# A two-layer streaming encoder on one core: select scratch and recurrence operands in PSUM, conditioning blocks moved

## Chip, cores and metric

The kernel runs on one core of one Trainium2 chip. The metric is the device time of one execution in microseconds (us), median of the runs; lower is better. The profile comes from one execution, recorded by the hardware profiler.

## What is computed

A prompt of 256 tokens and a sample of 32 tokens go through two layers of width 1024: a gated linear recurrence (layer 0) and a convolution module (layer 1), each followed by a PEER mixer that picks 16 of 16384 experts per head and token. Every part is normalised and modulated by a conditioning vector c. Cut to what matters:

```python
def rglru_block(h, ...):
    gate_branch, rec_branch = jnp.split(h @ w_in + b_in, 2, axis=-1)
    gate = jax.nn.gelu(gate_branch)
    xc = causal_dwconv(...rec_branch...)
    r, i = sigmoid(xh @ ga_w + ga_b), sigmoid(xh @ gx_w + gx_b)   # per head
    a = jnp.exp(-LRU_C * r * softplus(-lam))
    bvals = jnp.sqrt(1 - a * a) * (i * xc)
    hs = associative_scan(a, bvals)              # h[t] = a[t] h[t-1] + bvals[t]
    return (hs * gate) @ w_out + b_out

def peer(h, w_q, k1, k2, u, v):                  # per token, 8 heads
    s1, s2 = q1 @ k1.T, q2 @ k2.T                # 128 keys each
    s1v, s1i = top_k(s1, 16); s2v, s2i = top_k(s2, 16)
    sv, si = top_k(s1v[:, None] + s2v[None, :], 16)
    e = s1i[si // 16] * 128 + s2i[si % 16]
    g = softmax(sv)
    return sum(g * gelu(u[e] . h) * v[e])

for l in range(2):
    sh1, sc1, g1, sh2, sc2, g2 = split(silu(c) @ ada_w[l] + ada_b[l], 6)
    x = x + g1 * block(modulate(rmsnorm(x), sh1, sc1))
    x = x + g2 * peer(modulate(rmsnorm(x), sh2, sc2))
```

## The kernel before

The whole model runs on one core as a stream of items; `run_stream` (line 244) lays out one item per step `n`: a load on the SyncE (SP) queue, a split of the loaded tile into a rounded half `hi` (ScalarE, ACT) and a rest `lo` (VectorE, DVE, or GpSimd, POOL: `split_w`, line 329), and three groups of products on TensorE (PE): hi with both halves of the activations, lo with one (`mm3`, line 336). Splits run one step ahead, transposes of expert tiles two. Everything else (scans, top-16, gates, evictions) is in threads, lists of operations with an engine and a cost. `run_threads` (line 183) lets out as many of them per step as the engine's budget allows; a step's budget is the cost of its items on PE less what the split uses, and a conditioning block adds 0.5. So each engine's queue has a fixed order that the costs settle in advance. `drain_threads` lets out all that is left.

The order of items in layer 0: 16 conditioning blocks; 16 dense items for `w_in` (0 to 7 the recurrent half, 8 to 15 the gate half); 8 for `w_out`; then the PEER mixer: z items 0 to 127 (the product of all experts' `u` with the activations, with 16 query items between z1 and z8) and v items 0 to 127 (`v`). Layer 1 repeats this with its convolution in place of the recurrence. The names used below:

- A conditioning block is 512 KB of `ada_w`, four products with 32 columns of weights and 512 moving columns (`ada_unit`, line 390). Eight blocks make one of the twelve units (layer, part); the last block starts a small thread that transposes the row (ACT, PE) and adds the bias (DVE). `with_ada` hangs blocks behind items (`ride`) or ahead of one (`lead`). Blocks of layer 0's later units use a ring of nine buffers, so a block's load is issued when the block nine before it has been used.
- The recurrence ends in `lru_tail` (line 1368): per channel group c of 128, `ex` and `ex2` (exponential on ACT, square on POOL), `v1` (DVE), `sq` (square root, ACT), `v2` (a product and two scans, DVE), `gelu` (ACT) and `out` (product with the gate, POOL). `pre_wout` drains what is left and makes hi and lo of the result for `w_out`.
- After the query items, `select_ops` (line 738) finds the 16 best of 50 candidate pairs on DVE, turns their positions into two expert indices (`start1`, eight `steps`, `ints`, `start2`, eight `steps`), makes the softmax, and prepares tables for the gates (`tr`, `ev`, `parts`). Its work runs in both halves `hh` of 18 rows of 16. Beside it the z items go on: DVE transposes each tile of `u` (line 955), ACT makes hi, POOL makes lo while gates are open.
- PSUM has two pools of four banks: `bank()` for products, `bank(True)` for accumulators. `scr` and `big` are SBUF.

In `lru_tail` the order among roots and scans stands in these lines:

```python
sops += [("C", 0, lambda c=c: n["v1"] >= min(C, c // 4 * 4 + 4)), ("S", 0.33, lambda c=c: sq(c), 0)]
vops += [("C", 0, lambda c=c: n["sq"] > c), ("V", 0.95, lambda c=c: v2(c), 0)]
```

Of the kernel before, what the change touches and what calls it, by code (L numbers as in the profile page):

```python
# [21 lines left out]
P = 128  # L22
D = 1024
C = 8
# [22 lines left out]
def trunk_kernel(ctx: ExitStack, tc: tile.TileContext, I: dict, O: list):  # L47
# [564 lines left out]
    def peer_items(l, st, x8, sq8, hT8, hp8, rep8, ada_list):  # L612
# [125 lines left out]
        def select_ops():  # L738
            o = 4 * NA
            cand = scr[:, o:o + NH * NCAND].rearrange("p (h k) -> p h k", h=NH)  # L740
            ia, ib = hk(o, NA, I32), hk(o + NA, NA, I32)
            tmp = hk(o + 2 * NA, NA)
# [10 lines left out]
            def in_psum():  # L753
                return bank(True)[:, :NA].rearrange("p (h k) -> p h k", k=TOPK)
            bc = [P, NH // 2, TOPK]
            ops = []

            def add(eng, cost, fn, *hop):
                ops.append((eng, cost, fn) + hop)
# [10 lines left out]
            def conv():  # L770
                far["pos"], far["tmp"] = in_psum(), in_psum()
                for a in hh:
                    V.tensor_copy(far["pos"][:, a], ci[:, a])
                    V.tensor_copy(smx[:, a], sv[:, a, 0])
                for a in hh:
                    V.tensor_tensor(sv[:, a], sv[:, a], smx[:, a].unsqueeze(2).to_broadcast(bc), op=ALU.subtract)
            add("V", 1.1, conv)
            add("S", 0.5, lambda: S.activation(sv, sv, AF.Exp), 1)


            def start1():
                for a in hh:
                    V.tensor_copy(k1[:, a], idxs[0][:, a])
                for a in hh:
                    V.tensor_copy(k2[:, a], idxs[1][:, a])
                for a in hh:
                    V.scalar_tensor_tensor(k1[:, a], k1[:, a], 64.0, offs.unsqueeze(1).to_broadcast(bc),
                                           op0=ALU.mult, op1=ALU.add)
                for a in hh:
                    V.tensor_tensor(dl[:, a, 1:], k1[:, a, 1:], k1[:, a, :15], op=ALU.subtract)  # L790
                for a in hh:
                    V.tensor_copy(i1[:, a], k1[:, a, 0:1].to_broadcast(bc))
# [10 lines left out]
            add("V", 2.1, start1, 0)  # L803
# [3 lines left out]
            def soft():  # L807
                V.tensor_reduce(smx, sv, axis=AX.X, op=ALU.add)
                V.reciprocal(smx, smx)
                for a in hh:  # L810
                    V.tensor_tensor(sv[:, a], sv[:, a], smx[:, a].unsqueeze(2).to_broadcast(bc), op=ALU.mult)
            add("V", 1.2, soft, 0)

            def ints():
                for a in hh:
                    V.tensor_copy(ia[:, a], i1[:, a])
                for a in hh:
                    V.tensor_scalar(ib[:, a], ia[:, a], 63, None, op0=ALU.bitwise_and)
                for a in hh:
                    V.tensor_scalar(ia[:, a], ia[:, a], 6, None, op0=ALU.arith_shift_right)  # L820
                for a in hh:
                    V.tensor_copy(tmp[:, a], ib[:, a])

            def start2():
                for a in hh:
                    V.tensor_copy(i1[:, a], ia[:, a])
                for a in hh:
                    V.tensor_tensor(far["pos"][:, a], far["pos"][:, a], tmp[:, a], op=ALU.subtract)
                for a in hh:
                    V.tensor_tensor(dl[:, a, 1:], k2[:, a, 1:], k2[:, a, :15], op=ALU.subtract)  # L830
                for a in hh:
                    V.tensor_copy(i2[:, a], k2[:, a, 0:1].to_broadcast(bc))
# [5 lines left out]
            gate, man = scr[:, 4 * NP:5 * NP], scr[:, 5 * NP:6 * NP]  # L838
# [9 lines left out]
            def ev(tt):  # L848
                def f():
                    pt = st.pop(("slot", tt))  # L850
                    S.copy(sidx[:, :, tt * P:(tt + 1) * P], pt[:, :2 * P].rearrange("p (n t) -> p n t", n=2))
                    S.copy(gate[:, tt * P:(tt + 1) * P], pt[:, 2 * P:3 * P])
                return f

            def parts():
                V.tensor_copy(iota4, iota.unsqueeze(2).to_broadcast([P, P, 4]))
                V.tensor_scalar(man.bitcast(I32), gate.bitcast(I32), 0x007FFFFF, 0x44800000,
                                op0=ALU.bitwise_and, op1=ALU.bitwise_or)
                V.tensor_scalar(gate.bitcast(I32), gate.bitcast(I32), 0x7F800000, None, op0=ALU.bitwise_and)
                V.tensor_copy(smant[:, 0], man)  # L860
                V.tensor_scalar(sexp, gate, 1.0 / 1024, None, op0=ALU.mult)
# [506 lines left out]
    def lru_tail():  # L1368
# [12 lines left out]

        def sq(c):
            S.activation(ML[:, c, :], ML[:, c, :], AF.Sqrt)
            n["sq"] += 1

        def v2(c):
            V.tensor_tensor(IB[:, c, :], IB[:, c, :], ML[:, c, :], op=ALU.mult)
            V.tensor_tensor_scan(ML[:, c, :NP], RA[:, c, :NP], IB[:, c, :NP], 0.0, ALU.mult, ALU.add)
            V.tensor_tensor_scan(ML[:, c, NP:T], RA[:, c, NP:T], IB[:, c, NP:T], vc("state_lru_h", c),
                                 ALU.mult, ALU.add)  # L1390
            n["v2"] += 1
# [9 lines left out]
        for c in range(C):  # L1401
            sops += [("C", 0, lambda c=c: n["v1"] >= min(C, c // 4 * 4 + 4)), ("S", 0.33, lambda c=c: sq(c), 0)]
# [68 lines left out]
    with_ada(d, a01, {k: 2 for k in range(2, 10)}, {16: (8, 0)})  # L1471
    items += d
    a1 = ada_unit(0, 5, rc) + [it for u in range(2) for it in ada_unit(1, u, rc)]
# [441 lines left out]
```

## Time and profile before

| | us |
|---|---|
| Median of 3 runs | 2060.77 (2055.79 to 2065.05) |
| The profiled execution | 2065.36 |
| its span, first to last instruction | 2063.6 |
| PE busy | 1989.8 (96%) |
| DVE busy | 1534.8 (74%) |
| ACT busy | 1113.3 (54%) |
| POOL busy | 993.7 (48%) |

PE is the fullest engine over the whole span, but the shares are means over stages with different limits. What a change in one stage is worth is read from the windows and timelines of that stage: how much PE works in it, and for whom it waits. A timeline's bracket gives the idle time ahead of an instruction and who ended it; its durations are those of one instruction, or of a run of `x` equal ones. A long instruction can hide a wait of its own. The granted clock (PEclk) is a share of 2.4 GHz.

### The profile page before, as it was taken

Reading aid. Unit: us, or ns where it says so; the run is one execution under the profiler, and the core shown is the slowest. Engines: PE = TensorE matmul, PEld = TensorE weight load, DVE = VectorE, ACT = ScalarE, POOL = GpSimd, SP = SyncE. Lnnn points to the kernel's source line nnn. Section 1 sums busy time; section 2 is a strip of 40 time slices with the busy share of each in tenths; the row PEclk is TensorE's granted clock in tenths of the full one; section 3 lists DMA queues with packets and bytes.
Section 4 is the critical chain, followed back from the end, with each engine's and each line's share of the span. In section 5 each row is a group of like instructions: output and inputs, shape, how many; then the busy total and the mean of one; then the engine's idle time right before and its main releaser. Section 6 shows DMA issues by size and latency. Waiting matters only on the chain.

```text
span 2063.6 us, 38013 instructions
## 1 busy us (share of the span) xinstructions
PE 1989.8 (96%) x13603; PEld 1718.6 (83%) x13603; DVE 1534.8 (74%) x3324; ACT 1113.3 (54%) x1973; POOL 993.7 (48%) x644
## 2 busy tenths in 40 slices
PE   6989999999999999999999899999999999999998
PEld 4777978999999887777877679999999988777776
DVE  5785559999998876455658855799999978754455
ACT  3655434478886444344554544444888854444444
POOL 4346667777775232121245266877777743312100
PEclk9999999999999999999999999999999999999999
DMA  9856595555556988887686455665555578878863
GB/s 341 274 180 217 142 247 163 168 171 158 156 155 220 314 297 284 291 278 235 236 271 163 148 161 147 179 174 164 169 158 155 157 259 315 296 276 293 277 202 124
DMA packets 311483, 444.44 MB, mean 215 GB/s; under 512 B 29326, under 2 KB 248126, under 8 KB 310782
## 3 DMA queue, kind: packets, MB, share of 16 engines
q1 hardware_dynamic: 292142, 374.73, 57.6%
q0 software_dynamic: 18976, 67.22, 9.4%
q8 instruction: 107, 1.75, 0.4%
q14 instruction: 82, 0.67, 0.1%
q10 hardware_dynamic: 176, 0.07, 0.0%
HBM read 434.19 MB, written 4.87 MB: 213 GB/s over the span
## 4 chain that ended last, share of the span: by engine, by line
PE 65%; DVE 11%; issue 9%; DMA 8%; POOL 5%; ACT 2%; SPq 1%; DVEq 0%; ACTq 0%; POOLq 0%
PE b L342 34%; PE acc L1089 21%; DVE ut L955 3%; PE acc L913 3%; POOL scr L996 3%; POOL lo L333 2%; DMA raw<-in_peer_u_dram 2%; DMA raw<-in_peer_v_dram 2%; PE b L1033 1%; DMA big<-in_ada_w_dram 1%; DVE lo L333 1%; ACT hi L332 1%; PE acc L406 1%; DMA scr<-in_peer_u_dram,eidx 1%; DVE acc L798 1%
## 5 line engine op out<-in xcount | busy, mean ns | idle before, releaser
L342 PE MATMUL b<-rnd,hi 128*128 128x256 f32 (+1 forms) x5376 | 737.9, 290 | 19.7 <-ACT hi L332 10.8
L333 POOL TENSOR_TENSOR lo<-ut,hi 128x1024 fp32r<-128x1024 f32 x253 | 608.1, 2406 | 231.7 <-PE b L342 122.2
L342 PEld LDWEIGHTS b<-rnd,hi 128*128 128x128 f32 x5376 | 681.1, 190 | 42.2 <-ACT hi L332 15.8
L332 ACT CAST hi<-raw 128x1024 fp32r<-128x1024 f32 x336 | 353.1, 1052 | 396.7 <-DMA raw<-in_peer_v_dram 234.0
L1089 PE MATMUL acc<-hi,rnd 128*128 128x512 f32 x2048 | 557.6, 393 | 2.9 <-ACT hi L332 2.7
L333 DVE TENSOR_TENSOR lo<-raw,hi 128x1024 fp32r<-128x1024 f32 x282 | 348.1, 1236 | 265.0 <-PE acc L1089 124.7
L1089 PEld LDWEIGHTS acc<-hi,rnd 128*128 128x128 f32 x2048 | 380.2, 188 | 111.9 <-issue 23.4
L955 DVE STREAM_TRANSPOSE ut<-raw 128x1024 f32<-128x1024 f32 x256 | 317.0, 1239 | 129.4 <-DMA raw<-in_peer_u_dram 97.2
L342 PE MATMUL b<-rnd,lo 128*128 128x256 f32 (+1 forms) x2688 | 386.4, 285 | 9.6 <-POOL lo L333 5.2
L342 PEld LDWEIGHTS b<-rnd,lo 128*128 128x128 f32 x2688 | 351.2, 189 | 14.3 <-POOL lo L333 8.8
L332 ACT CAST hi<-ut 128x1024 fp32r<-128x1024 f32 x256 | 269.5, 1053 | 172.2 <-DVE ut L955 148.8
L1089 PE MATMUL acc<-lo,rnd 128*128 128x512 f32 x1024 | 317.7, 391 | 1.7 <-DVE lo L333 1.3
L1089 PEld LDWEIGHTS acc<-lo,rnd 128*128 128x128 f32 x1024 | 191.2, 188 | 46.6 <-DVE lo L333 6.8
L1023 POOL DMA_INDIRECT big<-in_peer_v_dram,eidx x64 | 65.6, 1025 | 266.0 <-PE b L1033 252.8
L333 POOL TENSOR_TENSOR lo<-raw,hi 128x1024 fp32r<-128x1024 f32 x54 | 129.9, 2407 | 113.0 <-PE b L342 60.1
L996 POOL DMA_INDIRECT scr<-in_peer_u_dram,eidx x64 | 84.2, 1316 | 187.3 <-DVE scr L1000 186.6
L907 ACT ACTIVATE scr<-scr 128x128 bf16<-128x128 bf16 x512 | 169.3, 407 | 0.0
L976 ACT ACTIVATE big<-b 128x512 f32<-128x512 f32 (+32 forms) x123 | 59.8, 486 | 73.4 <-PE b L342 73.2
L1000 DVE SCALAR_TENSOR_TENSOR scr<-scr 128x1024 f32<-128x1024 f32 x64 | 78.1, 1221 | 25.9 <-DMA scr<-in_peer_u_dram,eidx 25.7
L1064 DVE TENSOR_TENSOR rnd<-big,rnd 128x512 fp32r<-128x512 f32 x128 | 89.9, 702 | 4.1 <-ACT rnd L1063 4.1
L913 PE MATMUL acc<-scr 128*128 128x128 bf16 x1024 | 81.9, 223 | 0.0
L1063 ACT CAST rnd<-big 128x512 fp32r<-128x512 f32 x128 | 78.8, 615 | 4.0 <-PE b L342 4.0
(316 smaller groups left out, 1593.6 us busy)
## 6 DMA issues: line engine op xcount, KB each, us to landing
raw<-in_peer_u_dram SPq DMA_DIRECT2D x1024, 128.0 KB
raw<-in_peer_v_dram SPq DMA_DIRECT2D x256, 512.0 KB
big<-in_ada_w_dram SPq DMA_DIRECT2D x96, 512.0 KB
raw<-in_peer_w_q_dram SPq DMA_DIRECT2D x128, 128.0 KB
raw<-in_cf_w_pw_dram SPq DMA_DIRECT2D x24, 512.0 KB
raw<-in_lru_w_in_dram SPq DMA_DIRECT2D x16, 512.0 KB
raw<-in_lru_w_out_dram SPq DMA_DIRECT2D x8, 512.0 KB
xsave<-big SPq DMA_DIRECT2D x2, 1152.0 KB
```

Of the source, the lines that this page charges most:

```text
L332: S.copy(hi, src)
L333: (G if pool_lo else V).tensor_tensor(lo, src, hi.bitcast(F32), op=ALU.subtract)
L342: TE.matmul(ps, w[wi][:, c * P:(c + 1) * P], a[ai][:, c, :n], start=(start and wi == c == ai == 0), stop=(stop and wi == 1 and c == C - 1))
L907: S.activation(bt[:, j], b4[:, :, j], AF.Copy, scale=sexp[:, t0 + j:t0 + j + 1])
L913: TE.matmul(s["ps"][:, j * P:(j + 1) * P], a[:, :, j], bt[:, j], start=a is hi, stop=a is lo)
L955: V.transpose(s["ut"].rearrange("p (b e n) -> p e b n", b=8, e=4), s["raw"].rearrange("p (e b n) -> p e b n", e=4, b=8))
L996: G.indirect_dma_start(out=gt, out_offset=None, in_=Uf, in_offset=bass.IndirectOffsetOnAxis(ap=eidx[:, s:s + 1], axis=0))
L1000: V.scalar_tensor_tensor(gt, gt, 1.0, hs_v, op0=ALU.mult, op1=ALU.mult, accum_out=zs[:, s:s + 1])
L1023: G.indirect_dma_start(out=gt[j], out_offset=None, in_=Vf, in_offset=bass.IndirectOffsetOnAxis(ap=eidx[:, s + j:s + j + 1], axis=0))
L1063: S.copy(w[0], src)
L1064: V.tensor_tensor(w[1], src, w[0].bitcast(F32), op=ALU.subtract)
L1089: TE.matmul(acc[tt][half], w[a][:, c0:c0 + P], s["w"][b][:, half * 512:(half + 1) * 512], start=(i == 0 and a == 0 and b == 0), stop=(i == ...
```

## The change

It has three parts.

1. `select_ops`: scratch operands move into the two accumulator banks that the stage already holds (`pos` and `tmp`): the row maxima and the reciprocal sums (`red`), the scaled first index, the integer index (`int`), and later mantissa and exponent (`bits`). The casts of the indices to float go from DVE to ACT, behind the exponential; so does the iota copy of `parts`. The copy of the low index bits to float is dropped. `start1` is let out one step behind `exp` (hop 1).
2. `lru_tail`: `sq` writes its root into a bank of the product pool; `v2` multiplies in place there, and both scans read their second input from it. A root is let out only when the scan two channels before it has been.
3. Two more conditioning units (layer 0 part 5, layer 1 part 0) join the three that ride on the dense items of layer 0: two blocks behind items 2 to 9, 11, 13 and 15, four behind 10, 12 and 14, six instead of eight ahead of `w_out`. Eight blocks instead of 24 are left for the mixer of layer 0.

```diff
 def select_ops():
-            ia, ib = hk(o, NA, I32), hk(o + NA, NA, I32)
-            tmp = hk(o + 2 * NA, NA)
+            ib = hk(o + NA, NA, I32)
...
             def conv():
-                far["pos"], far["tmp"] = in_psum(), in_psum()
+                b0, b1 = bank(True), bank(True)
+                far["pos"], far["tmp"], far["int"] = in_psum(b0), in_psum(b1), in_psum(b1.bitcast(I32))
+                far["red"] = b0[:, NA:NA + NH]
+                far["bits"] = b0[:, :NP], b1[:, :NP]
                 for a in hh:
                     V.tensor_copy(far["pos"][:, a], ci[:, a])
-                    V.tensor_copy(smx[:, a], sv[:, a, 0])
+                    V.tensor_copy(far["red"][:, a], sv[:, a, 0])
                 for a in hh:
-                    V.tensor_tensor(sv[:, a], sv[:, a], smx[:, a].unsqueeze(2).to_broadcast(bc), op=ALU.subtract)
+                    V.tensor_tensor(sv[:, a], sv[:, a], red(a), op=ALU.subtract)
+
+            def exp():
+                S.activation(sv, sv, AF.Exp)
+                for n in range(2):
+                    S.copy(idxf[n], idxs[n])
             add("V", 1.1, conv)
-            add("S", 0.5, lambda: S.activation(sv, sv, AF.Exp), 1)
+            add("S", 1.3, exp, 1)
 
             def start1():
+                t = far["tmp"]
                 for a in hh:
-                    V.tensor_copy(k1[:, a], idxs[0][:, a])
-                for a in hh:
-                    V.tensor_copy(k2[:, a], idxs[1][:, a])
-                for a in hh:
-                    V.scalar_tensor_tensor(k1[:, a], k1[:, a], 64.0, offs.unsqueeze(1).to_broadcast(bc),
+                    V.scalar_tensor_tensor(t[:, a], k1[:, a], 64.0, offs.unsqueeze(1).to_broadcast(bc),
                                            op0=ALU.mult, op1=ALU.add)
                 for a in hh:
-                    V.tensor_tensor(dl[:, a, 1:], k1[:, a, 1:], k1[:, a, :15], op=ALU.subtract)
+                    V.tensor_copy(k1[:, a], t[:, a])
+                for a in hh:
+                    V.tensor_tensor(dl[:, a, 1:], t[:, a, 1:], k1[:, a, :15], op=ALU.subtract)
...
-            add("V", 2.1, start1, 0)
+            add("V", 1.6, start1, 1)
...
             def soft():
                 V.tensor_reduce(smx, sv, axis=AX.X, op=ALU.add)
-                V.reciprocal(smx, smx)
+                V.reciprocal(far["red"], smx)
                 for a in hh:
-                    V.tensor_tensor(sv[:, a], sv[:, a], smx[:, a].unsqueeze(2).to_broadcast(bc), op=ALU.mult)
+                    V.tensor_tensor(sv[:, a], sv[:, a], red(a), op=ALU.mult)
 
             def ints():
+                ia = far["int"]
...
-                for a in hh:
-                    V.tensor_copy(tmp[:, a], ib[:, a])
 
             def start2():
                 for a in hh:
-                    V.tensor_copy(i1[:, a], ia[:, a])
+                    V.tensor_copy(i1[:, a], far["int"][:, a])
                 for a in hh:
-                    V.tensor_tensor(far["pos"][:, a], far["pos"][:, a], tmp[:, a], op=ALU.subtract)
+                    V.tensor_tensor(far["pos"][:, a], far["pos"][:, a], ib[:, a], op=ALU.subtract)
...
             def ev(tt):
...
+                    if tt == 1:
+                        S.copy(iota4, iota.unsqueeze(2).to_broadcast([P, P, 4]))
 
             def parts():
-                V.tensor_copy(iota4, iota.unsqueeze(2).to_broadcast([P, P, 4]))
+                man, ex = far["bits"]
                 V.tensor_scalar(man.bitcast(I32), gate.bitcast(I32), 0x007FFFFF, 0x44800000,
                                 op0=ALU.bitwise_and, op1=ALU.bitwise_or)
-                V.tensor_scalar(gate.bitcast(I32), gate.bitcast(I32), 0x7F800000, None, op0=ALU.bitwise_and)
+                V.tensor_scalar(ex.bitcast(I32), gate.bitcast(I32), 0x7F800000, None, op0=ALU.bitwise_and)
                 V.tensor_copy(smant[:, 0], man)
-                V.tensor_scalar(sexp, gate, 1.0 / 1024, None, op0=ALU.mult)
+                V.tensor_scalar(sexp, ex, 1.0 / 1024, None, op0=ALU.mult)
                 V.tensor_tensor(smant[:, 1], man, smant[:, 0], op=ALU.subtract)
...
 def lru_tail():
+        pb = {}
+
         def sq(c):
-            S.activation(ML[:, c, :], ML[:, c, :], AF.Sqrt)
+            pb[c] = bank()[:, :T]
+            S.activation(pb[c], ML[:, c, :], AF.Sqrt)
             n["sq"] += 1
 
         def v2(c):
-            V.tensor_tensor(IB[:, c, :], IB[:, c, :], ML[:, c, :], op=ALU.mult)
-            V.tensor_tensor_scan(ML[:, c, :NP], RA[:, c, :NP], IB[:, c, :NP], 0.0, ALU.mult, ALU.add)
-            V.tensor_tensor_scan(ML[:, c, NP:T], RA[:, c, NP:T], IB[:, c, NP:T], vc("state_lru_h", c),
+            V.tensor_tensor(pb[c], IB[:, c, :], pb[c], op=ALU.mult)
+            V.tensor_tensor_scan(ML[:, c, :NP], RA[:, c, :NP], pb[c][:, :NP], 0.0, ALU.mult, ALU.add)
+            V.tensor_tensor_scan(ML[:, c, NP:T], RA[:, c, NP:T], pb[c][:, NP:T], vc("state_lru_h", c),
                                  ALU.mult, ALU.add)
...
-            sops += [("C", 0, lambda c=c: n["v1"] >= min(C, c // 4 * 4 + 4)), ("S", 0.33, lambda c=c: sq(c), 0)]
+            sops += [("C", 0, lambda c=c: n["v1"] >= min(C, c // 4 * 4 + 4) and n["v2"] >= c - 1), ("S", 0.33, lambda c=c: sq(c), 0)]
...
-    with_ada(d, a01, {k: 2 for k in range(2, 10)}, {16: (8, 0)})
+
+    a01 += ada_unit(0, 5, rb) + ada_unit(1, 0, rb)
+    with_ada(d, a01, {k: 4 if k in (10, 12, 14) else 2 for k in range(2, 16)}, {16: (6, 0)})
...
-    a1 = ada_unit(0, 5, rc) + [it for u in range(2) for it in ada_unit(1, u, rc)]
+    a1 = ada_unit(1, 1, rc)
```

## Rows read from the trace of the kernel before

**Rows 1.** The page, part 1: busy us, share of span, instructions.

```profile
PE 1989.8 (96%) x13603; PEld 1718.6 (83%) x13603; DVE 1534.8 (74%) x3324; ACT 1113.3 (54%) x1973; POOL 993.7 (48%) x644
```

**Rows 2.** Windows: us, busy by engine (x instructions), clock, DMA share, GB/s.

```profile
260.57:300.22 39.65, 38.97 (x299) 28.92 (x299) 19.77 (x77) 14.61 (x25) 24.89 (x19) 1.00 1.02 261
1290.80:1317.26 26.46, 26.46 (x224) 26.14 (x223) 19.34 (x73) 11.98 (x16) 21.99 (x13) 1.00 0.67 180
```

**Rows 3.** Windows around w_out of layer 0.

```profile
90.00:97.00 7.00, 7.00 (x57) 6.99 (x54) 5.79 (x10) 6.98 (x15) 6.56 (x8) 1.00 0.52 149
97.00:123.20 26.20, 18.23 (x132) 14.16 (x131) 25.85 (x40) 18.05 (x39) 15.62 (x12) 0.99 0.41 121
123.20:130.00 6.80, 6.79 (x41) 6.80 (x42) 4.94 (x15) 2.05 (x5) 0.00 (x0) 0.78 0.30 91
```

**Rows 4.** Timeline of DVE in the recurrence: start, us, line, operation [idle before].

```profile
100.34 0.45 DVE L1387 TENSOR_TENSOR big<-big 128x288 f32<-128x288 f32 x1
100.83 0.69 DVE L1388 TENSOR_TENSOR_SCAN big<-big 128x256 f32<-128x256 f32 x1
101.43 0.26 DVE L1389 TENSOR_TENSOR_SCAN big<-big,vecT 128x32 f32<-128x32 f32 x1
...
102.86 1.20 DVE L333 TENSOR_TENSOR lo<-raw,hi 128x1024 fp32r<-128x1024 f32 x1
...
115.04 2.76 DVE L1388 TENSOR_TENSOR_SCAN big<-big 128x256 f32<-128x256 f32 x1
...
119.45 2.29 DVE L1389 TENSOR_TENSOR_SCAN big<-big,vecT 128x32 f32<-128x32 f32 x1
```

**Rows 5.** Timeline of POOL in the recurrence.

```profile
111.31 0.87 POOL L1398 TENSOR_TENSOR big<-big 128x288 f32<-128x288 f32 x1 [1.36 <-ACT big L1416]
...
118.95 2.72 POOL L333 TENSOR_TENSOR lo<-raw,hi 128x1024 fp32r<-128x1024 f32 x1
```

**Rows 6.** Timeline of PE ahead of w_out.

```profile
115.32 3.64 PE L406 MATMUL acc<-big,scT 128*32 128x512 f32 x32
...
123.20 3.59 PE L342 MATMUL b<-rnd,hi 128*128 128x288 f32 x15 [3.92 <-DVE rnd L496]
```

**Rows 7.** Windows of the select stage: layer 0 in part, whole; layer 1.

```profile
326.00:371.00 45.00, 40.76 (x331) 39.30 (x329) 42.45 (x90) 21.16 (x24) 32.86 (x14) 1.00 0.57 162
326.00:433.00 107.00, 98.78 (x810) 95.86 (x809) 98.90 (x209) 48.96 (x65) 80.05 (x34) 1.00 0.57 164
1345.00:1450.00 105.00, 99.11 (x810) 96.82 (x808) 98.47 (x224) 49.17 (x65) 79.33 (x34) 0.98 0.60 168
```

**Rows 8.** Timeline of PE, select stage: a larger stall, one of ten small.

```profile
341.41 2.15 PE L342 MATMUL b<-rnd,hi 128*128 128x256 f32 x16 [1.86 <-ACT hi L332]
...
347.36 1.20 PE L342 MATMUL b<-rnd,lo 128*128 128x256 f32 x8 [0.32 <-POOL lo L333]
```

**Rows 9.** DVE by line and form, 290 to 450 us: busy us, mean ns.

```profile
L798 DVE SCALAR_TENSOR_TENSOR acc<-acc,scr 128x144 f32<-128x144 f32 x60 | 18.4, 308 | 1.5
...
L776 DVE TENSOR_TENSOR scr<-scr,smx 128x144 f32<-128x144 f32 x2 | 2.7, 1396 | 0.0
...
L818 DVE TENSOR_SCALAR scr<-scr 128x144 int32<-128x144 int32 x2 | 2.6, 1326 | 0.0
...
L859 DVE TENSOR_SCALAR scr<-scr 128x256 int32<-128x256 int32 x1 | 2.4, 2423 | 0.0
L856 DVE CAST scr<-iota 128x512 f16<-128x512 f32 x1 | 1.5, 1548 | 0.0
...
L773 DVE CAST acc<-scr 128x144 f32<-128x144 uint32 x2 | 0.6, 290 | 0.0
...
L783 DVE CAST scr<-scr 128x144 f32<-128x144 uint32 x2 | 0.3, 203 | 0.0
```

**Rows 10.** Windows of the projections ahead of that.

```profile
50.00:75.00 25.00, 25.00 (x170) 19.99 (x169) 22.08 (x47) 16.14 (x34) 10.47 (x21) 1.00 1.06 372
...
70.00:80.00 10.00, 10.00 (x69) 7.68 (x69) 9.47 (x23) 5.38 (x13) 0.95 (x1) 1.00 0.98 318
```

## What the change does to the time, and why

> **What bounds the kernel now.** I read the page's engine shares first: TensorE (PE) is busy 96% of the span [rows 1], so a gain has to come out of the 73.8 us in which PE stands idle, or out of work that PE no longer does. Then the windows, to see where the idle time lies, and for each stretch the timelines of the engines that PE waited for. Three stretches matter. (a) Nine z items behind the query projections of layer 0 carry conditioning blocks; the same nine of layer 1 carry none, and their windows stand side by side: 39.65 against 26.46 us [rows 2]. (b) Between the fifth gate product and w_out of layer 0, PE works 18.23 of 26.20 us, while VectorE (DVE) works 25.85 [rows 3]. The scans are the reason: a clean channel costs 0.45 + 0.69 + 0.26 us, but some scans take 2.76 or 2.29 us, and the last ends just behind a 2.72 us subtraction on GpSimd (POOL) [rows 4, 5]. PE waits 3.92 us for the last lo halves, and behind that wait the granted clock of 6.8 us is 0.78: part of them at the lower of its two levels, 1.2 GHz [rows 3, 6]. (c) In the select stage of both layers DVE is nearly full (42.45 of 45.00 us) and PE loses 8.22 us of 107 in layer 0 and 5.89 of 105 in layer 1, at a clock of 0.98 there [rows 7]. The larger losses stand behind ACT's hi cast, which waits for DVE's transpose; ten smaller ones, 0.3 us each, behind POOL's lo half [rows 8]. Which DVE instructions are long there is seen by line: 144 columns should take about 0.3 us, yet lines 776 and 818 average 1.4 and 1.3 us, and 859 takes 2.42 us for 256 columns [rows 9].
>
> **Part 1, the select stage, twice.** The slow forms are those whose operands all lie in SBUF. Line 798, with its output and first input in PSUM, is issued 60 times between POOL instructions that fill 32.86 of 45.00 us, and averages 308 ns: it never waits [rows 7, 9]. The change puts into PSUM an operand of just the lines that waited: the maxima and reciprocal sums (776, 811), the scaled first index (787, 790), the integers (816, 818, 820, 826), mantissa and exponent (857, 859). It takes the index casts (783, 785) and the copy of line 822 off DVE, and gives ACT those casts and the iota copy (856). In layer 0 that is 2.2 us at 776, 2.2 at 818, 2.1 at 859 and 1.5 at 856: 8 us by these four lines alone [rows 9]. PE can get back no more than it lost: 8.22 + 5.89, and 0.02 x 105 = 2.1 us for the clock, 16.2 us together. The sixteen long steps (lines 798 and 801) stay as they are; the ten small stalls, 3.2 us, are in them, and I let these and a little of the rest stay: **-12 us**. Bounds: -16, and -3 (the waits hop to operations that keep two SBUF operands, lines 830, 832 and 792). What is added: two casts and a copy on ACT, which is busy under half of these windows [rows 7]. Its next hi cast queues behind them, and start1 on DVE waits for them, for which the planner leaves one step (hop 1). I cost that at nothing; were that cover gone, it would be about the 1.5 us a layer that the iota copy took on DVE.
>
> A cast of 144 columns from SBUF to SBUF averages 203 ns, into PSUM 290 ns [rows 9]. The Trainium skill (VectorE: DVE Perf Modes, Why PSUM operands drop a tier) says that fp32 operations of one source lose their doubled rate once an operand is in PSUM; by that rule, with which these rows agree, some fourteen instructions a layer get slower. At 0.09 us each, were all of it on the path, the sum would be 2.4 us worse, but DVE has 8 us to spare by then.
>
> **Part 2, the conditioning blocks.** Sixteen of 24 blocks leave the z items of layer 0; one stays there, behind the seven ahead of the first. The two windows differ by 13.19 us for 17 blocks, with their transposes and two waits for DMA, so 16 blocks are worth 13.19 x 16/17: **-12.4 us** [rows 2]. Bounds -11 and -13.2. Each block takes with it its load on SP, its four products and an eighth of a post thread. The planner grants DVE 0.5 us per block, so without them the select thread runs slower: by the costs written in the code it starts its first top-16 two steps later and ends one step later, as layer 1 does today. The gates then end at z124, still ahead of the first v item, and the sample output one v item later, with room for it.
>
> The blocks go to the gate products: 18 more between items 10 and 15, two fewer ahead of w_out. A block costs PE between 0.45 us (eight in a row take 3.64 us [rows 6]) and 0.78 us (13.19/17, with a change of operand kind and the transposes). Here they come in twos and fours, and I take 0.6: 18 x 0.6 - 2 x 0.45 = 9.9 us. Against that stand 7.97 us of idle PE before w_out and 1.5 us that the clock of 0.78 takes out of the 6.8 us behind it [rows 3]. So PE alone would reach the end of w_out's first item 0.4 us later than today (from -2.3 at 0.45 a block to +3.7 at 0.78).
>
> **Part 3, the recurrence in PSUM.** Product and both scans now read one operand from PSUM, so by the argument of line 798 a channel should cost the clean 1.3 us. From 100.34 to 121.74 us, less three lo halves of 1.2 us, eight channels take 17.8 us today; 8 x 1.3 is 10.4 [rows 4]. DVE gains 7 us, and stops being what w_out waits for. What comes late next is PE with its blocks, then the loads. There is a price in order: root c may be issued only when scan c-2 has been, and ACT takes the gelus after all roots, so by the planner's order six of eight outputs on POOL fall behind the lo half of w_out's first tile and four behind that of its second, which waits for the buffer of the last gate product. After that product come 2.7 us of lo half [rows 5], then four outputs of 0.9 us [rows 5], then cast and lo half, some 7 us in all, and PE has six blocks and six transposes (4 us) to fill it, and its first channels of w_out for 2 us more. It just fits.
>
> **The loads.** In 90 to 123.2 us the DMA moves 149 GB/s x 7 + 121 x 26.2 = 4.2 MB [rows 3]; 16 blocks of 512 KB add 8.4 MB. 12.6 MB take 33.9 us at 372 GB/s, which it held from 50 to 75 us, and 39.6 at the 318 of 70 to 80 us [rows 10], against 33.2: +0.7 to +6.4. The last three blocks can only be asked for when item 14's are used. The Trainium skill (DMA: Bandwidth & Descriptors, Specifications) gives about 358 GB/s of HBM per core; by that figure an estimate is 35.2 us, or +2.0. The rows show more than that, so they decide.
>
> For what happens ahead of w_out together I take **+2 us**, between PE alone (+0.4) and the loads with their late requests; bounds -2.3 and +8.
>
> **The sum.** -12 - 12.4 + 2 = -22.4 us. The profiled execution took 2065.4 us, 4.6 above the median of the runs shown and just over their highest; against itself the sum gives 2043, against the median of 2060.8 it gives 2038.4. I predict **2038 us**.
>
> **The rivals.**
> *The wait moves (chance 0.12).* DVE keeps forms with two SBUF operands, and each can meet a POOL subtraction. For it: of the two instructions of line 776, and of 818, the means of 1.4 and 1.3 us say that only one waited [rows 9], so who waits is a matter of alignment. Against it: few of them are left per layer. Part 1 gives -3: 2047 us.
> *Loads too late (0.10).* If the DMA holds 318 GB/s with column slices and blocks mixed, w_out starts 6.4 us late and its own tiles come late behind it: +10 instead of +2: 2046 us.
> *A PSUM operand frees nothing (0.07).* Then the change doesn't do what it says: part 1 keeps only what leaves DVE (-3), the scans stay long, DVE ends as today at 122 us with two more units to finish, w_out +4: 2049 to 2051 us. Line 798 speaks against it. The Trainium skill (SBUF — State Buffer, Who interferes with whom) has it that a DVE instruction with at most one SBUF input, outside the doubled modes, does not contend with GpSimd; by that rule this rival is dead, and line 798's row agrees.
> *Slower: banks chain the engines (0.05).* Roots and gate products share four PSUM banks. As the steps run, product 13 takes the bank of channel 1, product 14 that of channel 3 and product 15 that of channel 5, each used at least one step before; root 3 waits for scan 0, root 7 for scan 4. If DVE falls more than a step behind, PE waits for scans, these for roots, and these queue on ACT behind evictions that wait for PE. Wholly in series, the stretch would take 25.85 + 18.05 + 18.23 = 62.1 instead of 26.2 us [rows 3], +36, and the sum becomes +11.6: 2072 us. It decides from 24.4 us of loss on. Against it: DVE has 7 us less to do in this stretch and PE 10 us more, so DVE should run ahead.
>
> **How the numbers follow.** My forecast has 0.66. Parts at their good ends give -16 - 13.2 - 2.3 = -31.5 (2029), at bad ends -3 - 11 + 8 = -6 (2055); runs of before spread by 5 us to either side. 2026 to 2052 leaves out the slower case, the worst of the bad ends and little below: two in ten. About 0.5%, or 10.3 us, is what a measurement of this kernel can tell from no change; faster means under 2050.5. Nearly all of the forecast lies there, and four fifths of the first two rivals: 0.81 faster; the third rival and the rests of the others make 0.14 within 0.5%; 0.05 slower.
>
> **What would show it.** Right: lines 776, 790, 818 and 859 of after near 0.3 us in both layers; no PE wait over 0.5 us in the select stage; z9 to z18 of layer 0 near 27 us; scans of 0.7 us while POOL is busy; DMA over 350 GB/s from 95 to 122 us; w_out starting between 121 and 127 us. Wrong: PE waiting for a PSUM bank or for blocks in items 12 to 15, a clock under 0.8 in w_out, or long DVE instructions at new lines of the select stage.

## The result, and the profile after

| | before | after |
|---|---|---|
| Median of 7 runs each, us | 2067.16 (2055.79 to 2067.98) | 2042.95 (2040.10 to 2046.96) |
| The profiled execution | 2065.36 | 2040.43 |
| its span | 2063.6 | 2038.7 |

The change makes the kernel faster: the ratio is 0.9894 (95% interval 0.9877 to 0.9912), some 22 us. The page of after, part 1, shows PE with 10.5 us less to do and 14.4 us less to wait than in [rows 1]:

```profile
PE 1979.3 (97%) x13603; PEld 1712.7 (84%) x13603; DVE 1519.0 (75%) x3314; ACT 1113.8 (55%) x1979; POOL 994.7 (49%) x645
```

Windows of after, with the columns of [rows 2]: three around w_out as in [rows 3], then the nine z items of layer 0 as in [rows 2].

```profile
90.00:97.00 7.00, 7.00 (x56) 5.40 (x55) 6.07 (x11) 6.98 (x15) 6.83 (x8) 1.00 0.71 222
97.00:123.20 26.20, 25.20 (x191) 17.38 (x191) 18.76 (x45) 18.00 (x43) 10.46 (x10) 1.00 1.05 390
123.20:130.00 6.80, 6.39 (x41) 3.98 (x36) 4.95 (x14) 2.63 (x6) 1.91 (x3) 1.00 0.67 209
262.36:290.47 28.11, 28.11 (x231) 26.82 (x231) 20.39 (x77) 12.68 (x20) 21.98 (x13) 1.00 0.59 166
```

Ahead of w_out PE now works 25.20 of 26.20 us, DVE 18.76 instead of 25.85, and the DMA moves 390 GB/s instead of 121; the granted clock behind it is 1.00, no longer 0.78. The nine z items of layer 0 take 28.11 instead of 39.65 us.

DVE by line and form in the select stage of layer 0 (busy us, mean ns):

```profile
L806 DVE SCALAR_TENSOR_TENSOR acc<-acc,scr 128x144 f32<-128x144 f32 x60 | 18.4, 307 | 1.5
...
L837 DVE TENSOR_TENSOR scr<-scr 128x135 f32<-128x135 f32 x2 | 3.7, 1914 | 0.0
L793 DVE SCALAR_TENSOR_TENSOR acc<-scr,offs 128x144 f32<-128x144 f32 x2 | 2.6, 1324 | 0.0
L880 DVE SCALAR_TENSOR_TENSOR scr<-scr 128x32 f32<-128x32 f32 x1 | 1.7, 1670 | 0.0
...
L827 DVE TENSOR_SCALAR scr<-acc 128x144 int32<-128x144 int32 x2 | 0.5, 303 | 0.0
L780 DVE TENSOR_TENSOR scr<-scr,acc 128x144 f32<-128x144 f32 x2 | 0.5, 300 | 0.0
L868 DVE TENSOR_SCALAR acc<-scr 128x256 int32<-128x256 int32 x1 | 0.4, 404 | 0.0
```

The lines that were long in [rows 9] (776, 818, 859; now 780, 827, 868) are short. Three others are long now: 793 and 837 (the old 787 and 830), and 880, the last sum. All three read two operands from SBUF. Each of them ends where a POOL subtraction ends. Line 837's two instructions and the two subtractions beside them, by the timelines of DVE and POOL:

```profile
369.62 3.75 DVE L837 TENSOR_TENSOR scr<-scr 128x135 f32<-128x135 f32 x2
```

```profile
368.40 4.82 POOL L333 TENSOR_TENSOR lo<-ut,hi 128x1024 fp32r<-128x1024 f32 x2 [0.95 <-ACT hi L332]
```

One pair ends at 373.37 us, the other at 373.22. Line 880 ends at 413.45 and the subtraction beside it at 413.40.

To compare kernels, each trace is cut at the same items. The table gives the steps as differences from before, in us. "w_out": from the start of the tenth item of w_in to that of w_out's second item. "z9 to z18" and "z18 to v" are in layer 0 (39.65 and 359.34 in before), "v items" goes from the first v item of layer 0 to the first dense item of layer 1 (392.67), "z9 to v, L1" is the same in layer 1 as the two together (382.02). The ratio is that of the times, with its interval, each against before on the same chip.

| kernel | w_out | z9 to z18 | z18 to v | v items | z9 to v, L1 | ratio |
|---|---|---|---|---|---|---|
| after | +2.2 | -11.5 | -7.0 | -5.9 | -3.8 | 0.9894 (0.9877, 0.9912) |
| after, again | +2.4 | -11.5 | -7.0 | -0.5 | -3.8 | 0.9886 (0.9868, 0.9903) |
| part 1 alone | 0.0 | +4.8 | -7.0 | -0.3 | -3.7 | 0.9956 (0.9942, 0.9970) |
| part 2 alone | +4.1 | -11.5 | -3.1 | -3.5 | +0.1 | 0.9926 (0.9903, 0.9948) |
| part 3 alone | -0.8 | -0.6 | -1.7 | +4.2 | +0.2 | 0.9983 (0.9965, 1.0002) |
| parts 2 and 3 | +2.4 | -11.5 | -3.1 | -7.0 | +0.1 | 0.9924 (0.9901, 0.9946) |
| ... and ACT's share of part 1 | +2.1 | -11.5 | -2.1 | -5.7 | +0.9 | 0.9947 (0.9928, 0.9965) |
| after, recurrence in SBUF | +2.7 | -11.5 | -7.1 | -5.1 | -3.8 | 0.9898 (0.9881, 0.9915) |
| after, lo halves on POOL | +2.3 | -11.5 | -7.7 | -6.2 | -3.8 | 0.9892 (0.9876, 0.9908) |
| ... and recurrence in SBUF | +3.7 | -11.5 | -7.7 | -4.1 | -3.8 | 0.9903 (0.9887, 0.9918) |
| after, more in PSUM | +2.3 | -11.5 | -11.3 | -2.5 | -8.0 | 0.9872 (0.9852, 0.9892) |
| after, more in PSUM, second | +2.3 | -11.5 | -11.5 | -6.5 | -8.2 | 0.9854 (0.9834, 0.9874) |

Where two kernels have the same code, z9 to z18 without blocks repeats within 0.1 us and the select stage of layer 1 within 0.2. That of layer 0 repeats within 0.7 us where the blocks are moved, and differs by 1.7 between before and part 3 alone. The v items and the z items with blocks vary by several us.

### The profile page after: what moved, and what is told of

It is laid out like the page before. It is cut to its first block, busy times and chain, and to the rows that moved or that the text cites. A ratio compares the mean times of both kernels' runs of the same rounds, so it can differ in the third digit from the quotient of the medians.

```text
span 2038.7 us, 38001 instructions
## 1 busy us (share of the span) xinstructions
PE 1979.3 (97%) x13603; PEld 1712.7 (84%) x13603; DVE 1519.0 (75%) x3314; ACT 1113.8 (55%) x1979; POOL 994.7 (49%) x645
## 4 chain that ended last, share of the span: by engine, by line
PE 72%; DVE 10%; DMA 6%; POOL 5%; issue 4%; ACT 2%; SPq 0%; DVEq 0%; POOLq 0%; ACTq 0%
PE b L342 34%; PE acc L1098 28%; DVE ut L964 4%; POOL lo L333 3%; PE acc L922 3%; DMA raw<-in_peer_u_dram 2%; PE b L1042 2%; POOL scr L1005 1%; DMA raw<-in_peer_v_dram 1%; PE acc L406 1%; ACT hi L332 1%; DMA big<-in_ada_w_dram 1%; DVE lo L333 1%; DVE acc L806 1%; PE b L712 1%
## 5 line engine op out<-in xcount | busy, mean ns | idle before, releaser
L342 PEld LDWEIGHTS b<-rnd,hi 128*128 128x128 f32 x5376 | 677.1, 189 | 29.5 <-issue 11.3
L985 ACT ACTIVATE big<-b 128x512 f32<-128x512 f32 (+16 forms) x124 | 60.2, 485 | 66.8 <-PE b L342 66.5
L1009 DVE SCALAR_TENSOR_TENSOR scr<-scr 128x1024 f32<-128x1024 f32 x64 | 78.2, 1222 | 24.8 <-DMA scr<-in_peer_u_dram,eidx 24.7
```

The source lines that it names most:

```text
L342: TE.matmul(ps, w[wi][:, c * P:(c + 1) * P], a[ai][:, c, :n], start=(start and wi == c == ai == 0), stop=(stop and wi == 1 and c == C - 1))
L1009: V.scalar_tensor_tensor(gt, gt, 1.0, hs_v, op0=ALU.mult, op1=ALU.mult, accum_out=zs[:, s:s + 1])
```

## The experiments: one part at a time

**Part 1 alone.** Before, with only the diff of `select_ops`.

> Only the select stage is changed (part 1), nothing else. Theory (operands in PSUM free DVE from POOL): the two select stages are shorter by what the trace of after shows between the z items and the first v item, 7.0 us in layer 0 and 3.8 in layer 1, so about -11 us in all, a ratio near 0.995; the prediction's own figure was -12. Rival (the wait moves to the forms that keep two SBUF operands): -3 us, a ratio near 0.9985.

Measured: 2055.53 us, ratio 0.9956, or 9.1 us. The steps of both select stages are those of after, 10.7 us together, as expected. Layer 0 as a whole gives only -2.2, since in this execution the blocks' loads in the z items came later than in before. The waits of PE (us in total, times, longest) from 260 to 306 us:

```profile
PE acc L406 <- DMA big<-in_ada_w_dram: 3.3, 6, 1.1
```

In before PE lost 0.7 us there in two such waits. So the z items with blocks vary with the DMA: 39.7, 44.5 and 39.0 us in the three kernels that keep them, 28.1 in all nine that don't.

**Part 2 alone.** Before, with only the last two hunks (`with_ada`, `a1`).

> Only the sixteen conditioning blocks are moved (part 2), the recurrence stays in SBUF. Both theories take -11.5 us from z9 to z18 of layer 0. Theory A (DVE's scans set the start of w_out, and the blocks fill PE's idle time there): w_out's first item starts at 123 to 125 us instead of 123.2, the total is -9 to -11. Theory B (without the recurrence's change, DVE ends later because it has two more units to finish): w_out starts at 127 us or later, the total is -7 or less.

Measured: 2048.95 us, ratio 0.9926, or 15.3 us: more than either theory. The z items give -11.5 and w_out's second item is 4.1 us late, so on those two theory B described the place (its first item starts at 127.83). The rest came from two stretches that no theory had named: 3.1 us between z18 and the v items, and the v items, which gave 3.5. DVE in the recurrence, 95 to 130 us:

```profile
L1388 DVE TENSOR_TENSOR_SCAN big<-big 128x256 f32<-128x256 f32 x8 | 9.5, 1193 | 0.3
...
L1387 DVE TENSOR_TENSOR big<-big 128x288 f32<-128x288 f32 x8 | 5.3, 667 | 0.0
L1389 DVE TENSOR_TENSOR_SCAN big<-big,vecT 128x32 f32<-128x32 f32 x8 | 4.1, 513 | 0.0
```

The eight channels still take 18.9 us, but PE works off the blocks beside them. From 115 us to w_out it waits longest for ACT's copy of a conditioning row:

```profile
124.30 0.44 PE L412 MATMUL acc<-ident,arow 128*128 128x128 f32 x2 [1.71 <-ACT arow L418]
```

**Part 3 alone.** Before, with only the hunks of `lru_tail`.

> Only the recurrence is changed (part 3: roots in PSUM banks, the order of roots), the blocks stay where they were. Theory (PSUM operands free the scans): DVE has 7 us less to do and w_out starts 3 to 5 us earlier than 123.2, with its clock back to 1.0: -4 to -6 us in all. Rival (the order puts gelus and outputs behind the roots, so POOL's tail of lo halves and outputs is late next): w_out starts within 1 us of 123.2, total within 1.5 us of no change.

Measured: 2063.33 us, ratio 0.9983 with 1 inside the interval (to 1.0002). The scans are clean (0.69 us), and w_out's first product starts at 118.97 instead of 118.89. PE's timeline behind it:

```profile
118.97 0.67 PE L342 MATMUL b<-rnd,hi 128*128 128x288 f32 x3
120.64 0.54 PE L342 MATMUL b<-rnd,hi 128*128 128x288 f32 x2 [1.00 <-DVE rnd L496]
121.61 0.54 PE L342 MATMUL b<-rnd,hi 128*128 128x288 f32 x2 [0.43 <-DVE rnd L496]
```

DVE's, and below it POOL's:

```profile
117.58 7.63 DVE L496 TENSOR_TENSOR rnd<-big,rnd 128x288 fp32r<-128x288 f32 x8 [1.31 <-ACT rnd L493]
```

```profile
120.23 3.92 POOL L1402 TENSOR_TENSOR big<-big 128x288 f32<-128x288 f32 x4
```

This is the rival's mechanism, at the place it named: the outputs on POOL fall behind, and the next DVE work with two SBUF inputs, line 496, runs beside them. Its eight pieces, duration in ns (least, median, most):

```profile
L496 DVE TENSOR_TENSOR rnd<-big,rnd x8: 444/1048/2630, 117.6 to 124.8; 128x288 fp32r<-128x288 f32 x8
```

One piece takes 2.63 us beside POOL's lo half, four take 1.05 beside the outputs (0.98 each), the other three 0.44 to 0.46. The eight take 3.03 us in before and 4.31 in after. So of the 8 us that the scans give back (11.1 instead of 19.0), line 496 takes 4.6.

**Parts 2 and 3, the select stage as before.**

> Parts 2 and 3 together, the select stage as before. Theory: -11.5 us (z items) + 2.2 us (w_out) = -9.3 us by the milestones of after; w_out starts at 126.3 us as in after. If this is close to part 2 alone, then part 3 gives nothing here; if it is some 4 us better than part 2 alone, part 3 pays for the blocks' place.

Measured: 2047.32 us, ratio 0.9924. This is part 2 alone within the intervals. In the trace, part 3 brings w_out's second item 1.7 us nearer (+2.4 instead of +4.1); in the time that can't be told from nothing. Against after, the select stage is the only difference: -7.0 less -3.1, and -3.8 less +0.1, is **-3.9 us a layer** for part 1. Against before, part 1 alone gave -7.0 and -3.7. The 3.1 us between the two in layer 0 are the same that the moved blocks gave there without part 1 (-3.1): which part they are counted to depends on which is taken first.

## The experiments: operand or order

In after, POOL has nothing to do while DVE scans. POOL's timeline:

```profile
94.08 4.24 POOL L1384 TENSOR_TENSOR big<-big 128x288 f32<-128x288 f32 x4
114.02 1.56 POOL L1411 TENSOR_TENSOR big<-big 128x288 f32<-128x288 f32 x2 [15.70 <-ACT big L1407]
115.62 2.40 POOL L333 TENSOR_TENSOR lo<-raw,hi 128x1024 fp32r<-128x1024 f32 x1
117.98 1.56 POOL L1411 TENSOR_TENSOR big<-big 128x288 f32<-128x288 f32 x2
```

The gelus come behind the roots, so the outputs do too. Clean scans in after (0.45 + 0.69 + 0.25 us) therefore don't show that a PSUM operand frees them. Three kernels tell the two apart:

```diff
# recurrence in SBUF, order of roots kept
-            S.activation(pb[c], ML[:, c, :], AF.Sqrt)
+            S.activation(ML[:, c, :], ML[:, c, :], AF.Sqrt)
-            V.tensor_tensor(pb[c], IB[:, c, :], pb[c], op=ALU.mult)
+            V.tensor_tensor(IB[:, c, :], IB[:, c, :], ML[:, c, :], op=ALU.mult)
...
# lo halves of the last four gate items on POOL
-        d.append(dense_item(w_in, c, gate_post(c)))
+        d.append(dense_item(w_in, c, gate_post(c), pool=c >= 4))
```

> The changed kernel with the recurrence's root, product and scan inputs back in SBUF, and the new order of roots kept. Theory (the PSUM operand frees the scans): scans are again 2 to 2.8 us where POOL works, and w_out starts 3 us or more later than 126.3. Rival (it is the order: gelus come after all roots, so POOL has nothing to do while DVE scans): scans stay at 0.69 and 0.26 us, w_out starts within 0.7 us of 126.3, and the time is within 1 us of the changed kernel's.

> The changed kernel, but the lo halves of the last four gate items are made by POOL, so that POOL subtracts (1.9 to 2.7 us each) while DVE scans operands in PSUM. Theory (a PSUM operand frees the scans): the scans of the channels beside POOL's lo halves stay at 0.69 and 0.26 us. Rival (a PSUM operand frees nothing): several of them take 1.5 to 2.8 us. The total isn't what this run is for; within 4 us of the changed kernel's.

> As the kernel with POOL's four lo halves, but with the recurrence's operands in SBUF. Theory (two SBUF operands wait for POOL): several scans or products take 1.5 to 2.8 us, w_out starts 2 to 5 us later than in the kernel that has them in PSUM. Rival (SBUF operands don't wait either): scans of 0.69 us in both.

Measured: 2040.25, 2038.70 and 2041.73 us, ratios 0.9898, 0.9892 and 0.9903. DVE in the recurrence, first with POOL's lo halves and operands in PSUM, then with POOL's lo halves and operands in SBUF:

```profile
L1401 DVE TENSOR_TENSOR_SCAN big<-big,b 128x256 f32<-128x256 f32 x8 | 5.5, 687 | 0.3
L1400 DVE TENSOR_TENSOR b<-big,b 128x288 f32<-128x288 f32 x8 | 3.6, 444 | 3.2 <-ACT b L1396 3.2
L1402 DVE TENSOR_TENSOR_SCAN big<-big,vecT,b 128x32 f32<-128x32 f32 x8 | 2.0, 254 | 0.0
```

```profile
L1399 DVE TENSOR_TENSOR big<-big 128x288 f32<-128x288 f32 x8 | 10.1, 1261 | 0.0
L1400 DVE TENSOR_TENSOR_SCAN big<-big 128x256 f32<-128x256 f32 x8 | 9.1, 1134 | 0.3
L1401 DVE TENSOR_TENSOR_SCAN big<-big,vecT 128x32 f32<-128x32 f32 x8 | 5.6, 703 | 0.0
```

Beside a busy POOL the eight channels take 11.1 us in PSUM and 24.8 in SBUF: the operand does free them. Without that load, with the new order, SBUF operands take 12.3 us:

```profile
L1400 DVE TENSOR_TENSOR_SCAN big<-big 128x256 f32<-128x256 f32 x8 | 6.2, 772 | 0.3
L1399 DVE TENSOR_TENSOR big<-big 128x288 f32<-128x288 f32 x8 | 3.5, 442 | 0.0
L1401 DVE TENSOR_TENSOR_SCAN big<-big,vecT 128x32 f32<-128x32 f32 x8 | 2.6, 321 | 0.0
```

So in the changed kernel the order does nearly all of it (18.9 us with the old order, in part 2 alone). Neither matters to the end: even the 24.8 us make w_out's second item only 1.4 us later, where 2 to 5 had been expected, and the three times lie together. What w_out waits for last in after, by PE's timeline, is the two last blocks:

```profile
124.09 1.05 PE L406 MATMUL acc<-big,scT 128*32 128x512 f32 x4 [0.23 <-DMA big<-in_ada_w_dram]
125.32 1.05 PE L406 MATMUL acc<-big,scT 128*32 128x512 f32 x4 [0.18 <-DMA big<-in_ada_w_dram]
```

## The experiments: what the select stage is worth

**Only the work that leaves DVE.** Parts 2 and 3, the casts and the iota copy on ACT and the dropped copy; nothing moved to PSUM.

```diff
             def start1():
-                for a in hh:
-                    V.tensor_copy(k1[:, a], idxs[0][:, a])
-                for a in hh:
-                    V.tensor_copy(k2[:, a], idxs[1][:, a])
...
+            def exp():
+                S.activation(sv, sv, AF.Exp)
+                for n in range(2):
+                    S.copy(idxf[n], idxs[n])
...
-                V.tensor_copy(iota4, iota.unsqueeze(2).to_broadcast([P, P, 4]))
```

> Parts 2 and 3, and of part 1 only what leaves DVE: the index casts and the iota copy go to ACT, one copy is dropped, start1 one step later; all scratch operands stay in SBUF. Counted from z18 of layer 0 and z9 of layer 1 to the first v item, parts 2 and 3 alone stand at -3.1 and +0.1 us against before, the whole change at -7.0 and -3.8. Theory (the banks make part 1's gain): within 1 us of -3.1 and +0.1, time about 2046. Rival (work taken off DVE makes it): -6 or less and -3 or less, time about 2042. It also bounds the prediction's -3 us for part 1 without PSUM.

Measured: 2052.28 us where the theory had 2046, ratio 0.9947, not faster than without it (0.9924). The select stages are 1.0 and 0.8 us longer than those of parts 2 and 3. DVE by line and form, layer 0, first in parts 2 and 3:

```profile
L826 DVE CAST scr<-scr 128x144 f32<-128x144 int32 x2 | 3.8, 1936 | 0.0
...
L785 DVE CAST scr<-scr 128x144 f32<-128x144 uint32 x2 | 2.6, 1330 | 0.0
...
L787 DVE SCALAR_TENSOR_TENSOR scr<-scr,offs 128x144 f32<-128x144 f32 x2 | 0.5, 294 | 0.0
L776 DVE TENSOR_TENSOR scr<-scr,smx 128x144 f32<-128x144 f32 x2 | 0.5, 292 | 0.0
...
L790 DVE TENSOR_TENSOR scr<-scr 128x135 f32<-128x135 f32 x2 | 0.5, 284 | 0.0
```

Then with that work off DVE (lines 787 and 790 are now 788 and 791):

```profile
L791 DVE TENSOR_TENSOR scr<-scr 128x135 f32<-128x135 f32 x2 | 2.7, 1386 | 0.0
L788 DVE SCALAR_TENSOR_TENSOR scr<-scr,offs 128x144 f32<-128x144 f32 x2 | 2.5, 1292 | 0.0
```

Line 776, 1396 ns in [rows 9], is short in both, and neither kernel changes the stage up to it. The long cast of line 785 is gone from DVE and that of line 826 is down to 738 ns (now 825), but lines 788 and 791, short before, are long in their place. Taking work off DVE gave nothing: which form meets a POOL subtraction is a matter of alignment, and some form does. This run also has the added casts and the copy on ACT; what they cost by themselves it doesn't show.

**More in PSUM.** After, with one input of each of the three long forms in a bank: ACT casts the first indices straight into `tmp` and writes a second copy of the second ones there.

```diff
-                for n in range(2):
-                    S.copy(idxf[n], idxs[n])
+                S.copy(far["tmp"], idxs[0])
+                for a in hh:
+                    S.copy(far["k2"][:, a], idxs[1][:, a])
+                S.copy(k2, idxs[1])
...
-                    V.scalar_tensor_tensor(t[:, a], k1[:, a], 64.0, ...
+                    V.scalar_tensor_tensor(t[:, a], t[:, a], 64.0, ...
-                    V.tensor_tensor(dl[:, a, 1:], k2[:, a, 1:], k2[:, a, :15], op=ALU.subtract)
+                    V.tensor_tensor(dl[:, a, 1:], far["k2"][:, a, 1:], k2[:, a, :15], op=ALU.subtract)
...
-                V.scalar_tensor_tensor(f(i2), f(i1), float(NKEY), f(i2), op0=ALU.mult, op1=ALU.add)
+                t = far["bits"][0][:, :2 * TOPK]
+                V.tensor_scalar(t, f(i1), float(NKEY), None, op0=ALU.mult)
+                V.tensor_tensor(f(i2), t, f(i2), op=ALU.add)
```

> The changed kernel, with the three forms of the select stage that kept two SBUF inputs and were seen long there (the scaled first index, the difference of the second indices, the last sum) given one input in PSUM: ACT casts the first indices straight into the bank and makes a second copy of the second ones there. Theory (the wait moved to these forms): their means fall from 1324, 1914 and 1670 ns to 0.3 us, and the time is 1 to 3 us below the changed kernel's. Rival (waits there are hidden, PE waits for ACT and POOL alone): same time within 1 us.

Measured: 2036.35 us, ratio 0.9872; each select stage is 4.2 to 4.3 us shorter than in after, more than expected. The copy behind the last sum, 32 columns within SBUF, now took long:

```profile
L894 DVE COPY gsel<-scr 128x32 f32<-128x32 f32 x1 | 1.3, 1347 | 0.0
```

The second version gives that copy to ACT and was measured beside after itself:

```diff
-                V.tensor_copy(gsel, f(sv))
+                S.copy(gsel, f(sv))
```

> The changed kernel with the three remaining forms of two SBUF inputs given one input in PSUM, as in the kernel with more PSUM operands, and the 32-column copy of the sample's gates, which took 1347 ns there, given to ACT. Theory (forms that read or copy within SBUF wait for POOL's subtractions): 4 to 6 us below the changed kernel measured beside it, no DVE instruction of the select stage over 0.7 us. Rival (the gain of the first such kernel was a matter of the run): within 1.5 us of the changed kernel.

> The changed kernel as it is, once more, as the measure for the next one and for what differs between executions of one kernel. The forecast parts should repeat within 0.5 us (w_out's second item +2.2, z9 to z18 -11.5, to the v items -7.0 in layer 0 and -3.8 in layer 1). Theory (the 5 us gained in layer 0's v items are late loads of v tiles, which come and go from run to run): that stretch differs from the first profile's -5.9 by 1 us or more. Rival (it belongs to the change): again -5 to -7.

Measured: 2033.42 us against after's 2040.34, ratios 0.9854 and 0.9886: 6.9 us by the medians, above the 4 to 6 expected, and the fastest kernel of the study. One DVE form is still long, so the expectation of none over 0.7 us failed. DVE by line and form in layer 0:

```profile
L895 DVE TENSOR_SCALAR eidx<-scr 128x32 uint32<-128x32 f32 x1 | 1.2, 1207 | 0.0
...
L848 DVE TENSOR_TENSOR scr<-acc,scr 128x135 f32<-128x135 f32 x2 | 0.5, 292 | 0.0
```

The wait hopped twice more, from the sum to the copy and from the copy to line 895, which took 169 ns in the first version. Both long instructions end within 0.1 us of the end of a POOL subtraction. The Trainium skill (SBUF — State Buffer, Who interferes with whom) says that copies, casts and `tensor_scalar`, with one input, can take the port pair shared with GpSimd too; the rows of lines 894 and 895 agree.

PE's waits in the select stage of layer 0 (us in total, times, longest), after, then the second version:

```profile
PE b L342 <- POOL lo L333: 2.9, 9, 0.3
PE b L342 <- ACT hi L332: 0.9, 1, 0.9
```

```profile
PE b L342 <- POOL lo L333: 1.0, 3, 0.3
```

Not only the larger stall goes: six of the nine small ones behind POOL go as well, though the long steps are as they were (308 ns each). Three are left in each layer in both versions; all the other traces have 5 to 10.

**Again after.** The forecast parts of after repeat within 0.2 us, but the v items of layer 0 stand at -0.5 instead of -5.9. PE's waits there: before, part 3 alone, after again; the first after has no such line.

```profile
PE acc L1089 <- ACT hi L332: 2.2, 2, 1.8
```

```profile
PE acc L1089 <- ACT hi L332: 5.6, 3, 4.2
```

```profile
PE acc L1098 <- DVE lo L333: 1.3, 4, 0.4
PE acc L1098 <- ACT hi L332: 1.0, 2, 0.6
```

ACT's hi cast stands there behind the loads of v tiles. These losses come and go in code that nobody touched: the same kernel gained 5.9 us there in one profile and 0.5 in the next, so one profile shows no gain of the change. Over all of them, the ten traces with the moved blocks stand at -4.7 us in the mean (-0.5 to -7.0), and the three without at 0.0, -0.3 and +4.2. So some of it may belong to the move. No run shows how, and that stays open.

## Why the prediction was right

The forecast, faster by 22.4 us, stands against 21.9 by the ratio (0.0106 x 2067). The median of before moved from 2060.8 to 2067.2 with more runs, which is why after's 2042.95 is 4.5 above the 2038 forecast. By its steps:

- **Part 1 was sized too large.** -12 forecast; by the traces -7.8 on top of parts 2 and 3 (3.9 a layer) and -10.7 alone, with the 3.1 us of layer 0 that can be counted to either part. The lines it moved became short, as said. But the first rival was partly true: the wait moved to line 830, which the prediction named there, to 787, of which the change moved only the output, and to the last sum. With these three given an operand in PSUM too, the stages give 8.4 and 8.3 us against parts 2 and 3: 16.7, just past the 16.2 that the prediction held to be the most PE can get back. So that bound was near the truth, and what kept the change from it were mainly these lines. "No PE wait over 0.5 us" failed by one of 0.9 and one of 0.6.
- **The ten small stalls were put down to the wrong cause.** The prediction let them stay "in" the long steps. Three are left when the last long forms go, against 5 to 10 in all other traces, while the steps stayed as they were. So the steps alone don't make them.
- **The third rival's price for work taken off DVE alone, -3, was wrong.** With the casts given to ACT it is +1.8 for both layers: the waits hop, and the run leaves open what ACT's new work adds.
- **Part 2 was right in place and nearly in size.** -11.5 for -12.4; 28.11 us for "near 27". Two things were missed: the items behind z18 gain 3.1 us by the traces of parts 2 and 2 with 3 (1.7 of which part 3 alone shows as well, so it is not firm), and with blocks in the z items their loads sometimes come 4.8 us later still. Both make part 2 worth more than forecast. Its 15.3 us alone also hold the v items (-3.5 in its trace), for which the prediction had no term.
- **Parts 2 and 3 ahead of w_out: +2 forecast, +2.2 and +2.4 measured.** PE became the bound with 25.20 of 26.20 us, the loads kept up at 390 GB/s (368 in after again) where the sum used 372, and the last two blocks wait 0.2 us each. POOL's tail "just fits" held with blocks to cover it; without them (part 3 alone) it doesn't, and line 496 pays. DVE's 7 us came as forecast (25.85 to 18.76; by the channels 18.9 to 11.1, that is 1.4 us for a clean one and not 1.3), and were worth 1.7 us at w_out and nothing measurable at the end. The reason given, that a PSUM operand frees the scans, is true by the pair with POOL's lo halves, but in this kernel the order alone brings most of it, since it leaves POOL idle.
- **The chained banks didn't come**: no wait of PE for a bank stands in items 12 to 15 of after.

By the steps of the traces: -7.8 - 11.5 - 3.1 + 2.3 = -20.1 us, and 21.9 by the times. The mechanisms of parts 1 and 2 are as forecast, that of part 3 only in part, and the sum looks better than its terms. With the 3.1 us counted to part 2, part 1 was too large by 4 and part 2 too small by 2; counted to part 1, both were too large by 1. What the times show beyond the steps had no term at all. That the total came within 0.5 us is luck in this.

## What to carry to other kernels

Where DVE and POOL ran side by side here, a DVE instruction at several times its usual length was waiting for a POOL instruction to end, and the wait belonged to the pair, not to the line: shortening or removing one such instruction moved it to the next. Give one input of every remaining form a place in PSUM, or look in the profile for the form that waits next, until none is left ahead of anything that PE needs. Work that an engine-bound stretch hides, like the blocks ahead of w_out, can be placed there before that stretch is made faster: here part 3 added nothing measurable to part 2.

## What the runs showed of the hardware

- A DVE form with two SBUF inputs and a POOL instruction with two wait for each other, and both sides lose. On DVE the same eight channels take 24.8 us beside POOL's subtractions, 11.1 with one operand in PSUM. On POOL an output takes 0.98 us beside line 496 (part 3 alone) and 0.78 in after (114.02 us).
- Forms with one input within SBUF wait as well: 1207 ns (line 895) and 1347 ns (the copy) for 32 columns that take 169 and 167 ns in other kernels of the study.
- The DMA held 390 GB/s over 26.2 us with column slices and 512 KB blocks mixed, 362 to 390 in the kernels with the moved blocks.
- The granted clock of 123.2 to 130 us is 1.00 in after, where no wait of PE ahead of it is over 0.6 us; 0.78 in before, behind the wait of 3.92 us [rows 6]; and 0.75 in part 3 alone, behind 1.00 us and four waits of 0.4 us. The last two hold some time at the lower level, 1.2 GHz. In part 2 alone it is 1.00, behind a wait of 1.71 us, so one wait of that length did not bring it down there.
